# Decays as steps of the written SSD order, transposed tiles scaled on VectorE from PSUM, and layer norm sums between the last group's steps

## The chip, the cores and the metric

The kernel runs on one core of a Trainium2 chip. The core has engines that each work through their own instructions in order and wait for one another by semaphores: TensorE (PE in the profile, with its weight loads shown as PEld), VectorE (DVE), ScalarE (ACT), GpSimd (POOL), and SyncE (SP), which issues most DMA transfers. The metric is the device time of one execution, in microseconds (us), lower being better. Matmuls write to PSUM, a small memory that DVE and ACT read; everything else on the chip lies in SBUF.

## The reference

One step of a decoder layer for 336 tokens of width 1024: a prompt of 272 (16 learned meta tokens and 256 new ones) and 8 running sequences of 8 tokens each (64 sample tokens). Cut to what this case touches:

```
proj = rmsnorm(x) @ w_in + b_in            # glu_in, z, xbc, dt, gates
u    = ga * sigmoid(gb)                     # conformer branch
c    = depthwise31(concat(cache, u))        # 31 taps per channel
y_a  = silu(layernorm(c)) @ w_conf_out + b_conf_out
xbc  = silu(depthwise4(concat(cache, xbc))) # x (32 heads x 64), B, C (8 groups x 128)
# SSD of a chunk, per group of 4 heads
decay  = exp(where(causal, acs[t] - acs[s], -inf))   # acs = cumsum(dt * A)
y_diag = (C @ B^T * decay) @ (dt * x)
y_off  = (C @ h) * exp(acs)
h      = exp(acs[last]) * h + B^T @ (exp(acs[last] - acs) * dt * x)
y   = (y_diag + y_off + D_skip * x) * silu(z)
y_b = group_rmsnorm(y) @ w_m_out
x   = x + (sigmoid(g_a) * y_a + sigmoid(g_b) * y_b) @ w_o
x   = x + peer(rmsnorm(x))                  # 8 heads x 16 of 16384 experts
```

The outputs are the tokens, the last 30 convolution inputs, the last 3 short convolution inputs and the SSD states.

## The kernel before

Activations lie transposed: channels on the 128 partitions, the 336 tokens in the columns (first the 64 sample tokens, then the 272 of the prompt). The prompt's tokens and the sample's are cut into three tiles, `TILES = ((0, 80), (80, 128), (208, 128))`: the first holds the sample and the 16 meta tokens, the others a chunk of 128 each.

**Projections.** One call of `proj` makes 128 output channels. It keeps 32-bit accuracy by splitting activations and weights into a high and a low part: 8 x 2 matmuls with the high weights `wh` on the parts `ah` and `al`, then 8 with the low weights `wl` on `ah`, 24 in all, into a PSUM buffer of tag pj (3 buffers). `weight` loads 512 KB (`wraw`, 4 buffers), casts it to `wh` on ACT (L214) and subtracts to `wl` on POOL (L215; of some weights on DVE), with 2 buffers each.

**Groups.** The SSD has 8 groups of 4 heads. For each group the main loop makes two projections of the Conformer branch (`conf`: value and gated), four of `xbc` (two of x, then B, then C, each followed by the short convolution and Silu) and two of `zproj` (Silu to `sz`). The long convolution of 31 taps (`conv_long`) runs its first tap on ACT (L391) and 30 on DVE (L393), on the prompt's and the sample's columns apart: 60 DVE instructions a group. The short one (`conv_short`) has one tap on ACT (L406) and three on DVE (L408).

**SSD steps.** `ssd(g, ...)` is a generator; the main loop advances it between projections, each `yield` being such a place:
- `turn(i)` transposes x and B of tile i on PE into a PSUM buffer of tag misc (ptr; the tag has 2 buffers, shared with pcb, pst, pq and the pst2 of `update`); ACT copies B out (L530) and scales x by dt in four pieces of 64 columns (L532); POOL makes `wx` of it.
- `inner(i)` makes C B^T (pcb), and DVE multiplies the decays `dec` with it in place (L545).
- `state(i)` makes the new chunk state: pst on PE; DVE copies it (tile 0, L553) or adds to it the old state times its decay, in four pieces (L557).
- `running()` reads the 8 sample states `st` (a DMA of 1 MB a group) into pq, and POOL scales `st` (eight products, L569). `update(q)` adds the new part to them: four matmuls into two PSUM buffers, then two additions on DVE (L599), in two steps, `update(0)` and `update(2)`.
- `out(b)` makes the output of two heads: py and po in PSUM buffers of tag y (2 buffers), then DVE (L585, L587, the latter with the growth factors `e2`) and POOL.
- The last step makes the sum of squares of the group norm: `sq` on ACT, one matmul (pgn), one addition on DVE (L641) to the running sum `pgn`.

**Decays.** `decays(g)` makes `dec` and `e2` of a group: for each of four heads two matmuls into a buffer of tag y (L498, L499), then three Exps on ACT, one a tile; then for each two heads two matmuls (L506) and an Exp (L195) to `e2`. It is called in the main loop between the first and the second xbc projection of the group, and before the loop for group 0. Its matmuls are not pinned.

**What sets the order.** `mm` and `tr` record a matmul or transpose and, inside the main loop, pin it to program order. Matmuls called directly are placed by the scheduler, which orders the rest by a simulated timeline and by priority. All table functions on ACT (Exp, Silu, Sigmoid, Ln; helper `act`, L195) are chained in program order, too, so that table loads are few. Where the next function lies in another table, an ACT_TABLE_LOAD stands between. The rest of DVE's, ACT's and POOL's work is ordered by the scheduler; the long convolution of groups after 0 has low priority.

**After the groups.** In the last group (g = 7) no further xbc projections follow; in their place `gate(0)` to `gate(5)` are projections of the gates, and the layer norm over the Conformer channels begins: `norm_mean` (a sum over the 8 tiles of `cbuf` by a matmul with ones, the eight subtractions on DVE, eight squares on ACT), `norm_var` (eight matmuls with ones) and `norm_scale` (rs on DVE and ACT, then eight products on DVE, L696, and eight Silus on ACT). `gnorm_stats` makes the factors of the group norm from `pgn` (Ln and Exp on ACT, short DVE steps); `gnorm` spreads them by a matmul with `id3` into pgb. Then come the output projections (`conf_out` first) and the expert mixer, which the diff does not touch.

## Time and profile before

| | |
|---|---|
| median of 3 runs | 1510.69 us (1509.24 to 1513.67) |
| profiled execution, its own time | 1508.3 us |
| span of its trace | 1506.5 us |
| mean granted TensorE clock | 0.957 |
| busy: PE | 1356.1 us (90%) |
| busy: PEld | 1272.0 us (84%) |
| busy: DVE | 1008.8 us (67%) |
| busy: ACT | 540.2 us (36%) |
| busy: POOL | 575.2 us (38%) |

Busy times are sums over the span of one profiled execution; the time of an execution is the span and a little around it (1508.3 - 1506.5 = 1.8 us). Rows of a group of instructions read "line engine operation out<-in, shape, count | busy us, mean ns of one | idle us of the engine ahead of them and what ended most of it". Rows of a timeline read "start us, duration us, engine, line, operation, shape, count", and in brackets how long the engine had waited and for whom. A granted clock of 1 is full speed. Tile names are cut to their letters in most rows (`id` is `id3` or `identb`, `acs` both the cumulated sums and their stacked form `acs3`).

### The profile page before, as it was taken

The page shows a single profiled execution, that of the slowest core. Times are in us where ns is not written, and L with a number is a line of the kernel's source. Part 1 is how long each engine was busy: PE and PEld are TensorE (multiplying, and loading weights), DVE is VectorE, ACT ScalarE, POOL GpSimd, SP SyncE. Part 2 cuts the span into 40 slices and gives each one's busy share as a digit, 9 for nine tenths or more (in the row PEclk, how much of TensorE's full clock was granted, in tenths as well). Part 3 has the DMA queues.
Part 4 walks back from the last instruction along what each step waited for, and adds up shares of the span by engine and source line. Part 5 has one row for each costly group of instructions (what it writes and reads, how often), then busy time and mean ns, then how long its engine had stood idle before and what let it go on. Part 6 is the DMA issues. An engine that isn't in the chain of part 4 may idle for free.

```text
span 1506.5 us, 24647 instructions
## 1 busy us (share of the span) xinstructions
PE 1356.1 (90%) x9308; PEld 1272.0 (84%) x9308; DVE 1008.8 (67%) x2350; ACT 540.2 (36%) x1441; POOL 575.2 (38%) x467
## 2 busy tenths in 40 slices
PE   5878877977979799999999988999988999987997
PEld 3767766866867699998989987999988999987997
DVE  6765675675582751256999997677788868776423
ACT  4666566576564744343422222112111101111001
POOL 2236545645656366575322133213223112242100
PEclk9879889989989899999999999999999999999999
DMA  5414234234333234444499989999999999999983
GB/s 192 153 61 158 83 120 165 74 133 144 106 127 113 74 131 148 142 143 158 141 394 414 414 331 416 415 403 364 417 380 417 409 368 375 383 417 416 413 333 104
DMA packets 86807, 382.05 MB, mean 254 GB/s; under 512 B 10112, under 2 KB 15360, under 8 KB 66080
## 3 DMA queue, kind: packets, MB, share of 16 engines
q1 hardware_dynamic: 64144, 226.87, 41.2%
q0 software_dynamic: 20736, 151.00, 24.6%
q10 hardware_dynamic: 1808, 2.60, 0.5%
q8 instruction: 73, 1.20, 0.3%
q14 instruction: 46, 0.38, 0.1%
HBM read 367.41 MB, written 13.03 MB: 253 GB/s over the span
## 4 chain that ended last, share of the span: by engine, by line
PE 49%; DVE 12%; DMA 7%; ACT 1%; issue 1%; POOL 0%; DVEq 0%; POOLq 0%; ACTq 0%
PE va L1277 18%; PE pj L150 14%; PE pj L1186 10%; PE pg L1215 4%; DMA eraw<-in_vE_dram 3%; DMA eraw<-in_uT_dram 3%; DVE ygat L1120 2%; DVE wuv L1112 2%; DMA nd<-x1d 1%; DVE si L922 1%; DVE cand L965 1%; PE psc L1022 1%; DVE si L919 0%; DVE cand L959 0%; DVE cand L962 0%
## 5 line engine op out<-in xcount | busy, mean ns | idle before, releaser
L1000 POOL DMA_INDIRECT wuv<-in_peer_uv_dram,gid x144 | 180.1, 1251 | 513.0 <-DVE ygat L1120 221.8
L215 POOL TENSOR_TENSOR wl<-wraw,wh 128x1024 fp32r<-128x1024 f32 x115 | 275.3, 2394 | 262.4 <-PE pj L150 125.5
L1186 PE MATMUL pj<-nd,eraw 128*128 128x176 f32 x2048 | 321.5, 316 | 12.0 <-DMA eraw<-in_uT_dram 9.1
L1277 PE MATMUL va<-S,eraw 128*128 128x176 f32 x2048 | 315.2, 314 | 12.7 <-DMA eraw<-in_vE_dram 12.7
L1186 PEld LDWEIGHTS pj<-nd,eraw 128*128 128x128 f32 x2048 | 308.0, 191 | 16.2 <-ACT S L1188 7.6
L1277 PEld LDWEIGHTS va<-S,eraw 128*128 128x128 f32 x2048 | 306.1, 190 | 17.6 <-DMA eraw<-in_vE_dram 15.9
L150 PE MATMUL pj<-ah,wh 128*128 128x336 f32 (+1 forms) x768 | 260.0, 346 | 2.1 <-ACT xnf L195 2.1
L150 PE MATMUL pj<-al,wh 128*128 128x336 f32 (+1 forms) x768 | 250.6, 333 | 0.0
L214 ACT CAST wh<-wraw 128x1024 fp32r<-128x1024 f32 x128 | 134.5, 1050 | 200.5 <-PE pj L150 120.9
L1120 DVE SCALAR_TENSOR_TENSOR ygat<-wuv,scg,ygat 128x1024 f32<-128x1024 f32 x128 | 164.0, 1281 | 50.8 <-ACT scg L1115 50.6
L1112 DVE SCALAR_TENSOR_TENSOR wuv<-wuv,x2m 128x1024 f32<-128x1024 f32 x128 | 156.0, 1219 | 40.2 <-DMA wuv<-in_peer_uv_dram,gid 40.2
L1114 ACT ACTIVATE scg<-scg 128x1 f32<-128x1 f32 x144 | 29.1, 202 | 411.5 <-DVE wuv L1112 411.4
L150 PEld LDWEIGHTS pj<-ah,wh 128*128 128x128 f32 x768 | 156.8, 204 | 15.1 <-issue 5.9
L150 PEld LDWEIGHTS pj<-al,wh 128*128 128x128 f32 x768 | 156.6, 204 | 1.0 <-DVE al L215 0.5
L393 DVE SCALAR_TENSOR_TENSOR pcv<-ccat,vec,pcv 128x272 f32<-128x272 f32 x464 | 146.6, 392 | 9.8 <-ACT pcv L391 9.8
L150 PE MATMUL pj<-ah,wl 128*128 128x336 f32 (+1 forms) x768 | 138.4, 319 | 0.0
L150 PEld LDWEIGHTS pj<-ah,wl 128*128 128x128 f32 x768 | 122.7, 189 | 0.8 <-issue 0.7
L1188 ACT ACTIVATE S<-pj 128x176 f32<-128x176 f32 x128 | 37.5, 311 | 148.0 <-PE pj L1186 148.0
L1215 PE MATMUL pg<-oh 128*128 128x64 bf16 x1056 | 75.7, 241 | 0.0
L1215 PEld LDWEIGHTS <-oh 128*128 128x128 bf16 x1056 | 71.2, 117 | 2.3
L1222 DVE TENSOR_TENSOR S<-S,pg 128x192 f32<-128x192 f32 (+1 forms) x66 | 31.6, 507 | 56.7 <-PE pg L1215 56.6
L498 PE MATMUL pdec<-acs,id 96*128 96x336 bf16 x32 | 11.9, 375 | 58.6 <-ACT dec L195 58.5
(345 smaller groups left out, 1750.4 us busy)
## 6 DMA issues: line engine op xcount, KB each, us to landing
eraw<-in_uT_dram SPq DMA_DIRECT2D x128, 512.0 KB, 13.2
eraw<-in_vE_dram SPq DMA_DIRECT2D x128, 512.0 KB, 9.3
wraw<-in_w_in_dram SPq DMA_DIRECT2D x80, 512.0 KB, 3.6
st<-in_state_dram SPq DMA_DIRECT2D x8, 1024.0 KB, 5.2
out_ssm_s_dram<-st SPq DMA_DIRECT2D x8, 1024.0 KB, 6.5
wraw<-in_w_mo_dram SPq DMA_DIRECT2D x16, 512.0 KB, 3.4
wraw<-in_w_q_dram SPq DMA_DIRECT2D x16, 512.0 KB, 3.4
wraw<-in_w_co_dram SPq DMA_DIRECT2D x8, 512.0 KB, 3.5
```

Of the source, the lines that this page charges most:

```text
L150: i_ = nc.tensor.matmul(*a_, **kw)
L214: (nc.vector.tensor_copy if on_dve else nc.scalar.copy)(h, src)
L215: (nc.gpsimd if on_pool else nc.vector).tensor_tensor(l, src, h.bitcast(F32), op=OP.subtract)
L393: t = nc.vector.scalar_tensor_tensor(o, i_, wv, a_, op0=OP.mult, op1=OP.add)
L1000: i_ = nc.gpsimd.indirect_dma_start(out=u, out_offset=None, in_=ia["peer_uv"], in_offset=bass.IndirectOffsetOnAxis(ap=gid[:, c:c + 1], axi ...
L1112: nc.vector.scalar_tensor_tensor(u[:, :D], u[:, :D], 1.0, x2m if c < NPICK else x2e, op0=OP.mult, op1=OP.mult, accum_out=w)
L1120: nc.vector.scalar_tensor_tensor(a_, u[:, D:], scg[:, c:c + 1], a_, op0=OP.mult, op1=OP.add)
L1186: i_ = nc.tensor.matmul(p[:, :ND], raw[:, k, :], nd[:, k, :], start=(k == 0), stop=(k == KD - 1))
L1188: nc.scalar.activation(Sv(b), p[:, :ND], AF.Gelu)
L1215: i_ = nc.tensor.matmul(pg[:, q, :], B[:, q // 4, :, q % 4], A[:, c_, q // 4, :, q % 4], start=(c_ == 0), stop=(c_ == 2))
L1222: nc.vector.tensor_tensor(sv_, sv_, pg.rearrange("p t i -> p i t")[:, i0:i1], op=OP.mult)
L1277: i_ = nc.tensor.matmul(va[k // 2][:, k % 2], raw[:, k, :], Sv(b), start=False, stop=(b == 127), skip_group_check=True)
```

## The change

1. **Decays.** `decays(g)` is gone. Its matmuls and Exps are now steps of `ssd(g)`: `decay(r)` for a head and `growth(b)` for two heads, their matmuls recorded with `mm` and so pinned. Decays 0 and 1 are the first step of a group, decays 2 and 3 come behind `turn(0)`, the growths behind `turn(1)` and `turn(2)`. `dec` and `e2` have one buffer in place of two.
2. **Steps.** The step list of a group is cut anew: decays 0, 1 | turn 0, decays 2, 3 | turn 1, 2, growths | running, inner 0 | inner 1, state 0 | inner 2, state 1, Bm | state 2, out 0 | out 1 | update 0 | update 2 | sum of squares. The main loop advances old and new group alike: the old group's `update(0)` and the new one's first step stand ahead of the value projection, then after each projection one step of each, as far as there are any.
3. **Transposed tiles.** The scaling of x by dt is one product on DVE that reads PSUM, 256 columns, with dt broadcast over 64 columns a head, in place of four ACT instructions. ACT still copies B out.
4. **States.** In `state(i)`, i > 0, POOL multiplies the old state with its decay, and one DVE addition of 256 columns adds PSUM, in place of four DVE instructions.
5. **Last group.** It takes the same steps; `norm_mean` comes before `gate(4)` as it did, `norm_var` is cut into two halves around `gate(5)`, `norm_scale` follows at once, then `gate(6)` and the group's last steps. `gnorm_stats` is called after the loop, and so behind the Silus of the layer norm in ACT's table order; it was called inside `norm_scale`, ahead of them.

```diff
 
-        def decays(g):
-            dec = sp.tile([128, 4, T], F32, name="dec", bufs=2)
-            e2 = sp.tile([128, 2, T], F32, name="e2", bufs=2)
-            for r in range(4):
-                h = 4 * g + r
-                pb = ps.tile([128, T], F32, name="pdec", tag="y", bufs=2)
-                nc.tensor.matmul(pb, id3[:, h:h + 1].to_broadcast([3 * H, 128]), acs3, start=True, stop=False)
-                nc.tensor.matmul(pb, identb, mneg, start=False, stop=True)
-                for i, (t0, L) in enumerate(TILES):
-                    act(dec[:, r, t0:t0 + L], pb[:, t0:t0 + L], AF.Exp, bias=acs[i][:, h:h + 1])
-            for b in range(2):
-                pb = ps.tile([128, T], F32, name="pdec", tag="y", bufs=2)
-                for r in range(2):
-                    h = 4 * g + 2 * b + r
-                    nc.tensor.matmul(pb[r * 64:(r + 1) * 64], id3[:, h:h + 1].to_broadcast([3 * H, 64]), acs3,
-                                     start=True, stop=True)
-                act(e2[:, b], pb, AF.Exp)
-            return dec, e2
-
         def r4(ap):
...
 
-        def ssd(g, xg, bc, sz, dec, e2):
+        def ssd(g, xg, bc, sz):
             BT, CT = bc[:, 0, :], bc[:, 1, :]
...
             xt, wx, hs = [], [], []
+            dec = sp.tile([128, 4, T], F32, name="dec")
+            e2 = sp.tile([128, 2, T], F32, name="e2")
+
+            def decay(r):
+                h = 4 * g + r
+                pb = ps.tile([128, T], F32, name="pdec", tag="y", bufs=2)
+                mm(pb, id3[:, h:h + 1].to_broadcast([3 * H, 128]), acs3, start=True, stop=False)
+                mm(pb, identb, mneg, start=False, stop=True)
+                for i, (t0, L) in enumerate(TILES):
+                    act(dec[:, r, t0:t0 + L], pb[:, t0:t0 + L], AF.Exp, bias=acs[i][:, h:h + 1])
+
+            def growth(b):
+                pb = ps.tile([128, T], F32, name="pdec", tag="y", bufs=2)
+                for r in range(2):
+                    h = 4 * g + 2 * b + r
+                    mm(pb[r * 64:(r + 1) * 64], id3[:, h:h + 1].to_broadcast([3 * H, 64]), acs3,
+                       start=True, stop=True)
+                act(e2[:, b], pb, AF.Exp)
 
...
                 nc.scalar.copy(x_[:L, 256:], p[:L, 256:])
-                for r in range(4):
-                    nc.scalar.activation(x_[:L, r * P:(r + 1) * P], p[:L, r * P:(r + 1) * P], AF.Copy,
-                                         scale=dtok[i][:L, 4 * g + r:4 * g + r + 1])
+                nc.vector.tensor_tensor(r4(x_[:L, :256]), r4(p[:L, :256]),
+                                        dtok[i][:L, 4 * g:4 * g + 4, None].to_broadcast([L, 4, P]), op=OP.mult)
                 w_ = sp.tile([128, 4, P], F32, name=f"wx{i}")
...
                 else:
-                    for r in range(4):
-                        c_ = slice(r * P, (r + 1) * P)
-                        nc.vector.scalar_tensor_tensor(h_[:, c_], hs[-1][:, c_], el[:, 8 + i, 4 * g + r:4 * g + r + 1],
-                                                       p[:, c_], op0=OP.mult, op1=OP.add)
+                    nc.gpsimd.tensor_tensor(r4(h_), r4(hs[-1]), decay_b(8 + i), op=OP.mult)
+                    nc.vector.tensor_tensor(h_, h_, p, op=OP.add)
                 hs.append(h_)
...
 
+            decay(0)
+            decay(1)
+            yield
             turn(0)
+            decay(2)
+            decay(3)
+            yield
             turn(1)
+            turn(2)
+            growth(0)
+            growth(1)
             for s_ in range(2):
...
             yield
-            turn(2)
+            running()
             inner(0)
...
             inner(1)
-            inner(2)
-            yield
             state(0)
-            running()
             yield
+            inner(2)
             state(1)
-            state(2)
-            nc.sync.dma_start(oa["ssm_p"][g], hs[2])
             Bm = sp.tile([S0, 4, N], F32, name="Bm")
...
             yield
+            state(2)
+            nc.sync.dma_start(oa["ssm_p"][g], hs[2])
             out(0)
...
 
-        def norm_var():
-            pv.append(pj())
-            for k in range(KD):
+        def norm_var(ks):
+            if not pv:
+                pv.append(pj())
+            for k in ks:
                 mm(pv[0], ones, squares[k], start=(k == 0), stop=(k == KD - 1))
...
             rstd_of(rs, pv[0], D, tp)
-            r24.append(gnorm_stats())
             for k in range(KD):
...
             f()
-        de = decays(0)
         lm[0] = LM[0]
...
         for g in range(G):
-            new = ssd(g, *tiles, sz, *de)
+            new = ssd(g, *tiles, sz)
             if g + 1 < G:
-                ca, cg = conf(g + 1)
-                ca()
-                run(old, 1)
-                run(new, 1)
-                cg()
-                run(old, 1)
-                run(new, 1)
                 tiles, steps = xbc(g + 1)
-                steps[0]()
-                run(new, 1)
-                de = decays(g + 1)
-                steps[1]()
-                run(new, 1)
-                steps[2]()
-                run(new, 1)
-                steps[3]()
+                tasks = conf(g + 1) + steps
+            else:
+                lm[0] = LM[1]
+                tasks = [lambda: gate(len(gates))] * 4
+            run(old, 1)
+            run(new, 1)
+            for f in tasks:
+                f()
+                run(old, 1)
                 run(new, 1)
+            if g + 1 < G:
                 sz, zsteps = zproj(g + 1)
...
                 zsteps[1]()
-                run(new, 1)
                 old = new
             else:
-                lm[0] = LM[1]
-                gate(0)
-                run(old, 2)
-                run(new, 2)
-                gate(1)
-                run(new, 2)
-                gate(2)
-                run(new, 1)
-                gate(3)
-                run(new, 1)
                 norm_mean()
...
                 run(new, 1)
+                norm_var(range(4))
+                run(new, 1)
                 gate(5)
                 run(new, 1)
-                norm_var()
-                run(new, 2)
+                norm_var(range(4, KD))
+                norm_scale()
+                gate(6)
+                run(new, 3)
         nc.scalar.dma_start(oa["mconv"], mnew)
...
         m2 = mix.enter_context(tc.tile_pool(name="m2", bufs=1))
-        norm_scale()
+        r24.append(gnorm_stats())
         while len(gates) < NB:
```

How this moves instructions shows in the order in which each engine takes them.

On PE the place is the start of a group, between its first Conformer projection (value, the rows ahead) and its second (gated, the rows behind). `pst` with a number is the `update(2)` of the group before, `ptr` the transposes of `turn(0)`, `pdec` the decays with their operands `id` and `mneg`. Before, the decays between them are two of the next group's, where the scheduler put them:

```order
L150 MATMUL pst_1269<-wx_734,Bm 128x256
L150 MATMUL pst_1270<-wx_734,Bm 128x256
L498 LDWEIGHTS id_256
L498 MATMUL pdec<-acs_247,id_256 128x336
L499 LDWEIGHTS identb
L499 MATMUL pdec<-mneg,identb 128x336
L498 LDWEIGHTS id_256
L498 MATMUL pdec<-acs_247,id_256 128x336
L499 LDWEIGHTS identb
L499 MATMUL pdec<-mneg,identb 128x336
L155 MATMUL ptr<-cst,xg 80x128 x2
L155 MATMUL ptr<-cst,bc 80x128
```

And of the change:

```order
L150 MATMUL pst_1239<-wx_712,Bm 128x256
L150 MATMUL pst_1240<-wx_712,Bm 128x256
L155 MATMUL ptr<-cst,xg 80x128 x2
L155 MATMUL ptr<-cst,bc 80x128
L150 LDWEIGHTS id_256
L150 MATMUL pdec<-acs_247,id_256 128x336
L150 LDWEIGHTS identb
L150 MATMUL pdec<-mneg,identb 128x336
L150 LDWEIGHTS id_256
L150 MATMUL pdec<-acs_247,id_256 128x336
L150 LDWEIGHTS identb
L150 MATMUL pdec<-mneg,identb 128x336
```

The transposes stand right behind the update now, where two decays stood between them; decays 2 and 3 stand behind the transposes.

On ACT the place is the decays' Exps. Before, they come behind the Silu of an xbc tile `xg`, whose short convolution begins with the first row:

```order
L406 ACTIVATE pj<-mcat,vec 128x360
L195 ACT_TABLE_LOAD
L195 ACTIVATE xg<-pj 128x272
L195 ACTIVATE xg<-pj 128x64
L195 ACT_TABLE_LOAD
L195 ACTIVATE dec<-pdec,acs_199 128x80
L195 ACTIVATE dec<-pdec,acs_224 128x128
L195 ACTIVATE dec<-pdec,acs_240 128x128
```

Of the change, `sz` being the output of a zproj projection and `xt` the copy of B in `turn(0)`:

```order
L195 ACTIVATE sz<-pj,vec 128x336
L637 ACTIVATE sq<-xg 128x336
L195 ACT_TABLE_LOAD
L195 ACTIVATE dec<-pdec,acs_199 128x80
L195 ACTIVATE dec<-pdec,acs_224 128x128
L195 ACTIVATE dec<-pdec,acs_240 128x128
L195 ACTIVATE dec<-pdec,acs_199 128x80
L195 ACTIVATE dec<-pdec,acs_224 128x128
L195 ACTIVATE dec<-pdec,acs_240 128x128
L214 CAST wh<-wraw 128x1024
L417 COPY ccat<-ccache 128x8x30
L529 COPY xt_1252<-ptr 80x128
```

The first two decays' Exps stand behind the last Silu of zproj and ahead of the copy of the first transposed B; those of decays 2 and 3 come after that copy.

On DVE the place is the end of a long convolution (L393) and the update of the states `st` behind it. Before:

```order
L587 TENSOR_TENSOR yo<-po,e_925 128x336
L599 TENSOR_TENSOR st<-st,pst_1794 128x512
L599 TENSOR_TENSOR st<-st,pst_1795 128x512
L599 TENSOR_TENSOR st<-st,pst_1833 128x512
L599 TENSOR_TENSOR st<-st,pst_1834 128x512
L641 TENSOR_TENSOR pgn<-pgn 8x336
L477 SCALAR_TENSOR_TENSOR ccat<-pj,vec,xnf 128x272
L478 SCALAR_TENSOR_TENSOR ccat<-pj,vec,xnf 128x8x8
L545 TENSOR_TENSOR dec<-dec,pcb 80x4x80
L393 SCALAR_TENSOR_TENSOR pcv<-ccat,vec,pcv 128x272
```

Of the change:

```order
L393 SCALAR_TENSOR_TENSOR cbuf<-ccat,vec,pcv 128x64
L595 TENSOR_TENSOR st<-st,pst_1790 128x512
L595 TENSOR_TENSOR st<-st,pst_1791 128x512
L530 TENSOR_TENSOR xt_1803<-ptr,dtok_193 80x256
L644 TENSOR_TENSOR pgn<-pgn 8x336
L477 SCALAR_TENSOR_TENSOR ccat<-pj,vec,xnf 128x272
L478 SCALAR_TENSOR_TENSOR ccat<-pj,vec,xnf 128x8x8
L530 TENSOR_TENSOR xt_1940<-ptr,dtok_218 128x256
L530 TENSOR_TENSOR xt_1949<-ptr,dtok_234 128x256
L393 SCALAR_TENSOR_TENSOR pcv<-ccat,vec,pcv 128x272
```

The three scaled tiles (L530) stand between the states' additions and the next convolution's first DVE step, and `inner(0)` (L545) has left this place.

More of the change, by code (lines that the diff above doesn't have):

```diff
@@ L610, in ssd @@
             inner(1)
+            state(0)
+            yield
             inner(2)
-            yield
-            state(0)
-            running()
-            yield
             state(1)
-            state(2)
-            nc.sync.dma_start(oa["ssm_p"][g], hs[2])
             Bm = sp.tile([S0, 4, N], F32, name="Bm")
@@ L730, in body @@
         for g in range(G):
-            new = ssd(g, *tiles, sz, *de)
+            new = ssd(g, *tiles, sz)
             if g + 1 < G:
-                ca, cg = conf(g + 1)
-                ca()
+                tiles, steps = xbc(g + 1)
+                tasks = conf(g + 1) + steps
[6 more added lines that the diff above has]
+                f()
                 run(old, 1)
                 run(new, 1)
-                cg()
-                run(old, 1)
-                run(new, 1)
-                tiles, steps = xbc(g + 1)
-                steps[0]()
-                run(new, 1)
-                de = decays(g + 1)
-                steps[1]()
-                run(new, 1)
-                steps[2]()
-                run(new, 1)
-                steps[3]()
-                run(new, 1)
+            if g + 1 < G:
                 sz, zsteps = zproj(g + 1)
```

## Prediction

> **What bounds the kernel now.** I read the busy times by stage first, then the waits of the groups, then the timeline of one group.
>
> ```profile
> span 1506.5 us, 24647 instructions
> 69.40:128.60 59.20, 46.68 (x287) 40.80 (x285) 39.45 (x117) 39.58 (x109) 28.25 (x30) 0.83 0.28 89
> 128.60:456.60 328.00, 276.26 (x1773) 236.42 (x1772) 207.23 (x573) 202.55 (x537) 179.65 (x173) 0.91 0.37 123
> 456.60:517.20 60.60, 47.85 (x298) 39.73 (x298) 30.28 (x58) 31.75 (x64) 31.67 (x25) 0.93 0.32 107
> 534.60:780.00 245.40, 239.97 (x1541) 233.02 (x1541) 139.27 (x466) 99.84 (x189) 134.21 (x75) 0.98 0.49 170
> 780.00:1506.50 726.50, 679.31 (x5076) 666.64 (x5074) 530.44 (x1013) 116.74 (x430) 174.90 (x138) 0.99 0.95 379
> ```
>
> The stage rows come from the view of busy times by stretch: length, then busy us of PE, PEld, DVE, ACT and POOL, the granted clock, the DMA share and GB/s. I cut where the second zproj projection of a group ends on PE. From 534.6 us on PE is busy 94 to 98% at a clock of 0.98 or more, and nothing of the diff runs there. What the diff touches lies before: group 0 (59.2 us), groups 1 to 6 (328.0 us, **54.67 each**) and group 7 with the norms. In groups 1 to 6 PE is busy 84%, at a clock of 0.91; DVE (63%), ACT (62%) and POOL (55%) are far from full. Something waits. The view of waits over the groups names it, the timeline tells why:
>
> ```profile
> PE pdec L498 <- ACT dec L195: 55.3, 7, 8.5
> 154.08 0.44 PE L498 MATMUL pdec<-acs,id 96*128 96x336 bf16 x1 [7.89 <-ACT dec L195]
> ...
> 146.63 0.65 ACT L406 ACTIVATE pj<-mcat,vec 128x360 f32<-128x360 f32 x1
> 151.38 0.51 ACT L195 ACTIVATE xg<-pj 128x272 f32<-128x272 f32 x2 [2.80 <-DVE pj L408]
> 151.89 1.28 ACT L195 ACT_TABLE_LOAD   x1
> 153.19 1.57 ACT L195 ACTIVATE dec<-pdec,acs 128x80 f32<-128x80 f32 x6
> ...
> 150.75 0.59 DVE L408 SCALAR_TENSOR_TENSOR pj<-mcat,vec,pj 128x360 f32<-128x360 f32 x1
> 151.25 8.90 DVE L393 SCALAR_TENSOR_TENSOR pcv<-ccat,vec,pcv 128x272 f32<-128x272 f32 x29
> ```
>
> PE's third decay matmul needs a buffer of tag y, and that comes free when ACT has exponentiated the first decay. ACT's table order puts this Exp behind the Silu of the xbc step just projected; the Silu waits for the short convolution on DVE (its last step at 150.75), and a table load follows. PE stands 7.89 us, seven times in all (55.3 us). It pays again afterwards:
>
> ```profile
> 156.89 0.65 PE L150 MATMUL pj<-ah,wh 128*128 128x336 f32 x1
> 162.65 0.69 PE L150 MATMUL pst<-wx,xt 16*128 16x256 f32 x2
> ...
> 184.46 0.42 PE L150 MATMUL pj<-ah,wh 128*128 128x336 f32 x1
> 188.37 1.13 PE L150 MATMUL pst<-wx,Bm 32*128 32x256 f32 x8
> 190.27 0.41 PE L155 MATMUL ptr<-cst,xg 128*80 128x128 f32 x2
> ```
>
> The projection after the stall takes 162.65 - 156.89 = 5.76 us, a later one 188.37 - 184.46 = 3.91, 0.16 us a matmul: 1.85 us more. The eight decay matmuls between stall and projection (154.08 to 156.89) take 2.81 us; at 0.15 each they would be 1.2: 1.6 more.
>
> **The change, part by part.** *Decays as pinned steps.* Decays 0 and 1 now follow the last zproj projection, and an update, the conf value projection, a second update and the first transposes come before decays 2 and 3 ask for the buffers. ACT reaches the Exps 0.5 (Silu of sz) + 1.28 (table) after that projection and is through both at 1.8 + 2 x 1.57 = 5 us. PE asks after 1.1 + 0.6 + 3.9 + 1.1 + 0.8 + 0.5 = 8 us. The stall is covered by 3 us, and with it goes the low clock: 7.89 + 1.85 + 1.6 = 11.3 per group. PE's own work is then 54.67 - 11.3 = **43.3 us**.
>
> What it adds is a wait: the first transposes follow update(2) at once, and need the buffer that DVE's addition to st frees. Today decays fill that gap; the update starts at 188.37, has 1.13 us, and ptr starts at 190.27: 0.8 us to wait, 44.1. Behind ptr on PE stand decays 2 and 3 and the gated projection.
>
> *What is late next* is a ring off PE: first transposes, ACT up to the start of the long convolution, its 60 steps on DVE, the additions to st behind them in DVE's order, the next transposes.
>
> ```profile
> 190.83 0.26 ACT L530 COPY xt<-ptr 80x128 f32<-80x128 f32 x1 [2.55 <-PE ptr L155]
> 198.62 0.44 ACT L391 ACTIVATE pcv<-ccat,vec 128x64 f32<-128x64 f32 x1
> L532 ACT ACTIVATE xt<-ptr,dtok 128x64 f32<-128x64 f32 x64 | 14.9, 328 | 0.0
> L195 ACT ACTIVATE e<-pdec 128x336 f32<-128x336 f32 x16 | 7.3, 455 | 1.9 <-PE pdec L506 1.9
> L557 DVE SCALAR_TENSOR_TENSOR hs<-hs,el,pst 128x64 f32<-128x64 f32 x64 | 13.3, 277 | 7.7 <-PE pst L150 7.7
> L545 DVE TENSOR_TENSOR dec<-dec,pcb 128x512 f32<-128x512 f32 x16 | 10.8, 681 | 5.0 <-PE pcb L150 5.0
> L553 DVE COPY hs<-pst 128x256 f32<-128x256 f32 x8 | 3.4, 424 | 8.3 <-PE pst L150 8.2
> L569 POOL TENSOR_TENSOR st<-st,el 128x256 f32<-128x256 f32 x64 | 36.9, 615 | 0.0
> ```
>
> From ptr (190.27) to the end of the second pcv start (199.06) pass 8.8 us now. Out go twelve scaled copies (14.9/64 each: 2.8); in come two pairs of Exps (3.1), a table load (1.28) and two e2 Exps (0.9): 11.3. Then DVE: 60 steps at 8.90/29 = 0.307 (18.4), twelve short steps at the 0.5 from 150.75 to 151.25 (6.0), three products with dec (two at 0.68, a smaller one some 0.5: 1.85), a copy and two state additions (3 x 0.42), four output operations on 336 columns (some 0.52 each, between 0.42 and 0.68: 2.1), two additions to st (512 columns, 1.35): 31.0. With 0.8 for the addition that frees the buffer the ring takes 43.1 us, against 44.1 on PE. PE stays the bound, by one microsecond, and DVE's order puts the end of the convolution just ahead of that addition. I add 0.9 us for short waits (an estimate; bounds 0 and 3.9, one projection held back once a group): **45.0 us per group**.
>
> *Transposed tiles on VectorE, states with GpSimd.* ACT loses L532, counted above. DVE loses eight L557 (13.3/64 each: 1.7) and gains three products and two additions on 256 columns. The trace has no product from PSUM with such a broadcast; its bounds are the 0.42 of L553 and the 0.68 of L545, 2.1 to 3.4 for five. I take 0.42, the same number of columns. The three products come before the convolution starts, so 1.3 to 2.0 beside ACT's work there: 0, with +2 a group if that cover is gone. The states' products cost POOL 2 x 0.615, and POOL is idle 24 us in a group. DVE's addition waits for them, with convolution steps queued behind it; by the order they stand behind a weight split on POOL that ends, by my count, 1.5 us before DVE asks. Cost 0, bounds 0 and +1.5.
>
> *Group 0.*
>
> ```profile
> 72.70 0.44 PE L498 MATMUL pdec<-acs,id 96*128 96x336 bf16 x1 [3.12 <-ACT dec L195]
> 75.50 0.65 PE L150 MATMUL pj<-ah,wh 128*128 128x336 f32 x1
> 80.93 0.38 PE L155 MATMUL ptr<-cst,xg 128*80 128x128 f32 x2
> ```
>
> It holds the decays of groups 0 and 1 now. Out: 8.5, 1.85 and 1.6 as above, the second set's own 1.8, the 3.12 shown, 1.6 on its decays and 5.43 - 3.91 = 1.5: 20.0. In: two decays that lie before 69.4 now (0.6) and 1.7 of waits. 59.2 becomes 41.5, a gain of **17.7**.
>
> *Group 7 and the norms.*
>
> ```profile
> 465.91 0.44 PE L155 MATMUL ptr<-cst,xg 128*128 128x128 f32 x2 [0.49 <-ACT xt L532]
> 468.03 0.40 PE L150 MATMUL pcb<-bc 128*80 128x80 f32 x2 [1.57 <-ACT xt L532]
> 468.19 0.60 PE L150 MATMUL pj<-ah,wh 128*128 128x336 f32 x1
> 473.51 0.60 PE L150 MATMUL pcb<-bc 128*128 128x128 f32 x4
> 488.17 6.33 DVE L696 TENSOR_TENSOR cbuf<-cbuf,rs 128x336 f32<-128x336 f32 x8 [1.04 <-ACT rs L694]
> 504.38 0.73 PE L150 MATMUL pgn<-sq,cstm 128*8 128x336 f32 x2 [0.87 <-DVE st L599]
> 517.21 0.72 PE L150 MATMUL pgb<-acs,id 96*128 96x336 bf16 x2 [8.18 <-DVE acs L225]
> ```
>
> In: its own decays (1.8), the ptr wait (0.8). Out: the waits on L532 (0.49 + 1.57) and the slow projection behind them (473.51 - 468.19 - 3.91 = 1.4). The eight subtractions (6.33) now stand on DVE ahead of a dec product that PE needs: +1.3 by my count. The norm's 16 sum matmuls cost what they cost. The stall before pgb stays, and its cover goes: gate(6) ran inside it, now it runs ahead, and ACT has its evacuation (0.5), a table load, eight Silus (some 0.55 each) and two more loads with Ln and Exp (3.5) to do before nine short DVE steps (4.4): 14.1 us from gate(6)'s end to pgb, 2.9 of them PE's work. That is 11.2 idle against 0.87 + 8.18 now: +2.2. Together **+2.6**, bounds -3 and +6.
>
> **Sum.** 17.7 + 6 x (54.67 - 45.0) = 58.0, less 2.6: 73 us. The profiled execution took 1508.3 us (its span and 1.8 around it): 1435. The median of the runs, 1510.69, lies 2.4 above it: **1437**.
>
> [...]
>
> **Rivals.** *(a) New waits in the ring.* ACT and DVE run in a fixed order, one microsecond off the path; one late cast or weight split moves all. At 48 us a group: 14.7 + 6 x 6.67 - 2.6 = 52, **1458**. For it the thin margin, against it that ACT idles 20 us in a group. *(b) Short waits in a cluster lower the clock,* as at 468: 1.4 us in each of seven groups, 10, **1447**. *(c) The stall only moves:* the Silu of C's tile holds the Exps at the new place, too. It would have to be late by 3 us after two further projections to be seen, by 11 to undo the gain: **1510**. *(d) Slower.* DVE's state addition waits for POOL's product, which stands behind weight splits and the eight products with st (8 x 0.615 = 4.9 us); taps, short steps and so Silus and pj buffers stand behind the addition. Each microsecond beyond the 1.5 of cover costs one in each of seven groups. The gain is gone at 10.4; with 13 it is 18 us slower, **1529**. POOL's 24 idle us speak against it.
>
> **Chances.** Forecast 0.64 (own range 1428 to 1447), (a) 0.20, (b) 0.08, (c) 0.04, (d) 0.03, 0.01 for anything else. The range 1424 to 1463 takes in (a) and (b), and at its low end a ring without any wait (44.1, 5 us less) and a group 7 that gains. A measurement of this kernel tells 0.3% (4.5 us) from no change: faster 0.93, same 0.04, slower 0.03.
>
> **What would show it.** Right: no wait of several us at pdec; 45 us from a group's first update to the next group's; 3.9 us for every projection; a granted clock near 1 in groups 1 to 6; 8 to 12 idle us before pgb. Wrong: a period of 48 or more, with PE waiting for a cast, a weight split or a product on DVE; projections of 5 us; or a stretch from the first conf_out to the end that is not 972 us long.

## The result and the profile after

| | before | after |
|---|---|---|
| median | 1510.24 us (4 runs) | 1431.84 us (1431.42 to 1433.83, 4 runs) |
| ratio to before | | 0.948, 95% interval 0.9462 to 0.9497 |
| profiled execution, span | 1506.5 us | 1430.0 us |
| mean granted clock | 0.957 | 0.974 |
| busy PE, DVE, ACT, POOL | 90, 67, 36, 38% | 93, 70, 37, 41% |

The kernel is 78.4 us faster. The view of busy times by stretch, cut at the same events as before (at the end of the second zproj projection that comes ahead of each of groups 0, 1 and 7, at the first pgb and at the first conf_out), shows where. At the first cut the first decay starts in the changed kernel; in the kernel before, two decays (0.6 us) lie ahead of it. The columns are those of the prediction's first fence.

```profile
0.00:72.10 72.10, 51.80 (x259) 42.09 (x260) 49.54 (x104) 36.69 (x87) 16.97 (x21) 0.91 0.49 167
72.10:111.30 39.20, 39.20 (x280) 36.06 (x279) 32.48 (x93) 31.20 (x79) 27.60 (x30) 1.00 0.39 122
111.30:372.40 261.10, 255.29 (x1772) 224.48 (x1772) 204.73 (x562) 190.43 (x467) 188.13 (x188) 1.00 0.47 156
372.40:444.00 71.60, 51.39 (x310) 41.52 (x310) 37.02 (x71) 42.58 (x82) 32.04 (x27) 0.84 0.27 91
444.00:460.80 16.80, 14.75 (x80) 13.87 (x80) 12.93 (x25) 8.94 (x19) 9.66 (x8) 0.86 0.18 53
460.80:1430.00 969.20, 922.18 (x6616) 903.61 (x6614) 670.42 (x1477) 215.99 (x617) 307.91 (x211) 0.98 0.84 327
```

| stretch | before | after | measured | forecast |
|---|---|---|---|---|
| up to group 0 | 69.4 | 72.1 | +2.7 | 0 |
| group 0 | 59.2 | 39.2 | -20.0 | -17.7 |
| groups 1 to 6 | 328.0 | 261.1 | -66.9 | -58.0 |
| group 7, norms, pgb | 78.0 | 88.4 | +10.4 | +2.6 |
| from conf_out on | 971.9 | 969.2 | -2.7 | 0 |

In groups 1 to 6 PE is busy 98% now and its clock is 1.00 throughout. DVE, ACT and POOL are busy there about as long as before (205, 190 and 188 us in place of 207, 203 and 180, the difference being the moved products); what has gone is idle time. The last group got much longer, at a granted clock of 0.84.

The waits of the groups (us in total, times, the longest) hold no row for pdec any more. What PE itself still waits for there are two rows:

```profile
PE ptr L155 <- DVE st L595: 4.6, 6, 0.8
PE ptr L155 <- DVE pgn L644: 0.6, 1, 0.6
```

And this is one group boundary in the timeline, PE first, then ACT, then DVE (start, length, and in brackets the wait and its releaser):

```profile
155.77 0.32 PE L150 MATMUL pdec<-acs,id 96*128 96x336 bf16 x1
...
160.17 1.13 PE L150 MATMUL pst<-wx,Bm 32*128 32x256 f32 x8
162.08 0.42 PE L155 MATMUL ptr<-cst,xg 128*80 128x128 f32 x2 [0.78 <-DVE st L595]
162.44 0.31 PE L150 MATMUL pdec<-acs,id 96*128 96x336 bf16 x1
...
154.91 0.52 ACT L195 ACTIVATE sz<-pj,vec 128x336 f32<-128x336 f32 x1
155.44 1.28 ACT L195 ACT_TABLE_LOAD   x1
156.73 1.58 ACT L195 ACTIVATE dec<-pdec,acs 128x80 f32<-128x80 f32 x6
...
158.87 0.68 DVE L393 SCALAR_TENSOR_TENSOR cbuf<-ccat,vec,pcv 128x272 f32<-128x272 f32 x2
161.33 1.29 DVE L595 TENSOR_TENSOR st<-st,pst 128x512 f32<-128x512 f32 x2 [1.78 <-PE pst L150]
162.93 0.42 DVE L530 TENSOR_TENSOR xt<-ptr,dtok 80x256 f32<-80x256 f32 x1 [0.31 <-ACT xt L529]
```

Three things are to be read here. The Exps of decays 0 and 1 end at 158.31, and PE asks for their buffer at 162.44: the stall is covered by 4.1 us. The only wait left here is the 0.78 us of the first transposes for DVE's addition. And DVE ends the long convolution at 159.55, then itself waits 1.78 us for PE's pst: DVE is that far from being the bound here. It is so at five of the seven boundaries; at the first and the sixth DVE waits only 0.26 and 0.57 us.

The last group's timeline, PE first, then DVE:

```profile
406.65 0.70 PE L150 MATMUL pst<-wx,xt 128*128 128x256 f32 x2 [2.10 <-DVE dec L543]
409.83 0.48 PE L150 MATMUL pj<-al,wh 128*128 128x336 f32 x1
421.69 1.13 PE L150 MATMUL pst<-wx,Bm 32*128 32x256 f32 x8
427.83 2.67 PE L150 MATMUL pst<-wx,Bm 32*128 32x256 f32 x8 [5.00 <-DVE st L595]
444.01 0.72 PE L150 MATMUL pgb<-acs,id 96*128 96x336 bf16 x2 [11.96 <-DVE acs L225]
...
398.44 7.55 DVE L699 TENSOR_TENSOR cbuf<-cbuf,rs 128x336 f32<-128x336 f32 x8 [1.39 <-ACT rs L697]
421.59 5.59 DVE L714 TENSOR_TENSOR cbuf<-cbuf,rs 128x336 f32<-128x336 f32 x8
427.10 1.27 DVE L595 TENSOR_TENSOR st<-st,pst 128x512 f32<-128x512 f32 x2
```

`update(0)` ends on PE at 422.82, but DVE has just begun the norm's eight products (421.59, 5.59 us) and adds to `st` only at 427.10. `update(2)` needs the PSUM buffers that this addition frees: 5.00 us. Ahead of it, the eight subtractions hold a decay product back (2.10 us), and before pgb PE stands 11.96 us.

In the kernel before, DVE took these products (L711 there) behind the additions to `st`:

```profile
504.57 0.68 DVE L599 TENSOR_TENSOR st<-st,pst 128x512 f32<-128x512 f32 x1
...
506.78 3.42 DVE L711 TENSOR_TENSOR cbuf<-cbuf,rs 128x336 f32<-128x336 f32 x8
```

They took 3.42 us there. The view of the tile (ns of one: least, median, most) and GpSimd's timeline show where the other 2.2 us of the 5.59 come from:

```profile
L714 DVE TENSOR_TENSOR cbuf<-cbuf,rs x8: 494/496/2652, 421.6 to 426.7; 128x336 f32<-128x336 f32 x8
421.90 2.40 POOL L215 TENSOR_TENSOR wl<-wraw,wh 128x1024 fp32r<-128x1024 f32 x1 [1.88 <-ACT wh L214]
```

One product, from 422.01 to 424.66, took 2.65 us, the others half a microsecond. It falls together with GpSimd's split of the weight for gate(6), which the change has put ahead of the last steps. The same holds for one of the eight subtractions, 2.65 us beside a split at 403.28, and for one in the kernel before, 2.68 us beside a split at 491.76. That the split causes it was not tried by itself.

### The profile page after: what moved, and what is told of

Its sections match the earlier page's. It is cut to its first block, busy times and chain, and to the rows that moved or that the text cites. A ratio compares the mean times of both kernels' runs of the same rounds, so it can differ in the third digit from the quotient of the medians.

```text
span 1430.0 us, 24506 instructions
## 1 busy us (share of the span) xinstructions
PE 1334.6 (93%) x9308; PEld 1261.6 (88%) x9308; DVE 1007.1 (70%) x2326; ACT 525.8 (37%) x1347; POOL 582.3 (41%) x483
## 4 chain that ended last, share of the span: by engine, by line
PE 51%; DVE 13%; DMA 6%; ACT 1%; POOL 0%; issue 0%; DVEq 0%; ACTq 0%
PE va L1267 19%; PE pj L150 14%; PE pj L1176 12%; PE pg L1205 5%; DMA eraw<-in_vE_dram 3%; DVE ygat L1110 2%; DVE wuv L1102 2%; DMA eraw<-in_uT_dram 2%; DVE si L912 1%; DVE cand L955 1%; DMA nd<-x1d 1%; PE psc L1012 1%; DVE si L909 1%; DVE cand L949 1%; DVE cand L952 1%; DVE ci L909 0%
## 5 line engine op out<-in xcount | busy, mean ns | idle before, releaser
L1176 PEld LDWEIGHTS pj<-nd,eraw 128*128 128x128 f32 x2048 | 311.5, 193 | 13.8 <-ACT S L1178 8.5
L150 PE MATMUL pj<-ah,wh 128*128 128x336 f32 (+1 forms) x768 | 250.0, 334 | 2.4 <-ACT xnf L195 2.1
L150 PE MATMUL pj<-al,wh 128*128 128x336 f32 (+1 forms) x768 | 241.3, 322 | 0.0
L1110 DVE SCALAR_TENSOR_TENSOR ygat<-wuv,scg,ygat 128x1024 f32<-128x1024 f32 x128 | 163.9, 1280 | 53.4 <-ACT scg L1105 53.2
L393 DVE SCALAR_TENSOR_TENSOR pcv<-ccat,vec,pcv 128x272 f32<-128x272 f32 x464 | 151.7, 388 | 17.9 <-ACT pcv L391 17.9
L150 PEld LDWEIGHTS pj<-ah,wh 128*128 128x128 f32 x768 | 148.5, 194 | 12.2 <-issue 4.4
L150 PEld LDWEIGHTS pj<-al,wh 128*128 128x128 f32 x768 | 148.7, 194 | 1.1 <-DVE al L215 0.5
L408 DVE SCALAR_TENSOR_TENSOR pj<-mcat,vec,pj 128x360 f32<-128x360 f32 x96 | 56.4, 587 | 0.5 <-ACT pj L406 0.3
```

What stands on the lines that cost most here:

```text
L150: i_ = nc.tensor.matmul(*a_, **kw)
L393: t = nc.vector.scalar_tensor_tensor(o, i_, wv, a_, op0=OP.mult, op1=OP.add)
L408: nc.vector.scalar_tensor_tensor(o, cat[:, w:w + n], wv, o, op0=OP.mult, op1=OP.add)
L1110: nc.vector.scalar_tensor_tensor(a_, u[:, D:], scg[:, c:c + 1], a_, op0=OP.mult, op1=OP.add)
L1176: i_ = nc.tensor.matmul(p[:, :ND], raw[:, k, :], nd[:, k, :], start=(k == 0), stop=(k == KD - 1))
```

## The experiments

Each kernel was timed against the kernel before on the same chip, so the ratios can be compared. The parts of the span that no kernel here edits vary from kernel to kernel: the first decay starts on PE between 68.8 and 72.1 us, and the stretch from the first expert matmul to the end takes 749.3 to 755.8 us. So beside the times stands, for kernels made from the changed one, the **middle stretch** between these two places, 679.6 - 72.1 = 607.5 us in the changed kernel.

### One call moved in the kernel before

```diff
                 steps[0]()
                 run(new, 1)
-                de = decays(g + 1)
                 steps[1]()
...
                 zsteps[1]()
                 run(new, 1)
+                de = decays(g + 1)
                 old = new
```

> The kernel before with one call moved: the decays of the next group are recorded behind its last zproj projection, not between its first two xbc projections; nothing else of the change. Theory A (the gain comes from the place of the Exps in ACT's table order; the rest of the change adds little): the stall of 7.9 us at the third pdec goes; since all six decay buffers now follow one another on PE, short waits of 0.8 to 1.5 us for each Exp set take its place, some 4 us a group; a period of 47 to 50 us, 1460 to 1480 us. Theory B (the new cut of the steps, VectorE and GpSimd carry a good part): the stall only moves, a period of 52 us or more, over 1490 us.

Measured: 1460.1 us, ratio 0.9662 (0.9646 to 0.9678). The period is 47.9 us (pq of group 1 at 143.82, of group 6 at 383.32, five periods). PE at the decays, then in the projection behind them, and the stretches around them with their clock:

```profile
214.63 0.30 PE L498 MATMUL pdec<-acs,id 96*128 96x336 bf16 x1 [1.10 <-ACT dec L195]
215.36 0.30 PE L498 MATMUL pdec<-acs,id 96*128 96x336 bf16 x1 [0.28 <-ACT dec L195]
216.09 0.33 PE L506 MATMUL pdec<-acs,id 96*64 96x336 bf16 x2 [0.28 <-ACT dec L195]
216.83 0.33 PE L506 MATMUL pdec<-acs,id 96*64 96x336 bf16 x2 [0.40 <-ACT dec L195]
217.60 0.48 PE L150 MATMUL pj<-ah,wh 128*128 128x336 f32 x1
```

```profile
214.00:217.10 3.10, 1.50 (x9) 0.62 (x8) 3.10 (x10) 3.10 (x13) 1.11 (x2) 1.00 0.49 166
217.10:220.60 3.50, 3.50 (x15) 3.50 (x14) 0.06 (x1) 0.75 (x3) 0.96 (x2) 0.54 0.11 37
```

One line of the old kernel, with no other part of the change, brings 51 of the 78 us: theory A. The third pdec waits 1.10 us in place of 7.9. What this kernel lacks against the change is also in the rows: four waits of 2.06 us together, and a projection of 5.51 us in place of 3.99, since the clock falls to 0.54 for 3.5 us. That is 3.6 of the 4.4 us between the two periods. The changed kernel, with the decays spread over three places of the step order, shows neither; the spreading alone was not tried. Fewer table loads are not the cause of the gain: this kernel has 27 ACT_TABLE_LOADs at L195 in place of 34, but the changed kernel has 36 and is faster.

### The decays alone put back

```diff
-            decay(0)
-            decay(1)
             yield
             turn(0)
-            decay(2)
-            decay(3)
...
-            growth(0)
-            growth(1)
...
             for n_, f in enumerate(tasks):
+                if n_ == 3 and g + 1 < G:
+                    de = decays(g + 1)
                 f()
```

with `decays(g)` as it was, two buffers each.

> The changed kernel with the decays alone as they were: one function, unpinned, recorded between the first two xbc projections, two buffers each; steps, VectorE scaling, GpSimd states and the last group as in the change. Theory A: the stall of some 7 us at the third pdec is back in each group, with slower projections behind it; a period of 53 to 55 us, 1495 to 1510 us. Theory B: the other parts hold their share, a period under 50 us, below 1475 us.

Measured: 1507.09 us, ratio 0.997 (0.9955 to 0.9986), a period of 53.2 us (pq at 145.46 and 464.92, six periods). PE's third decay, and ACT around it:

```profile
207.03 0.44 PE L498 MATMUL pdec<-acs,id 96*128 96x336 bf16 x1 [6.58 <-ACT dec L195]
...
204.32 0.51 ACT L195 ACTIVATE xg<-pj 128x272 f32<-128x272 f32 x2 [2.04 <-DVE pj L408]
204.84 1.28 ACT L195 ACT_TABLE_LOAD   x1
206.13 1.58 ACT L195 ACTIVATE dec<-pdec,acs 128x80 f32<-128x80 f32 x6
```

The stall is back, with the same neighbours as before: the Exp stands behind the Silu of an xbc tile, and that behind DVE. Steps, VectorE and GpSimd without the decays' new place leave 4 us of the 78. Together with the first experiment this settles what the gain hangs on: the place alone brings 51 us, the rest alone 4, and the other 23 come only with both.

### The transposed tiles on ACT again

```diff
-                nc.vector.tensor_tensor(r4(x_[:L, :256]), r4(p[:L, :256]),
-                                        dtok[i][:L, 4 * g:4 * g + 4, None].to_broadcast([L, 4, P]), op=OP.mult)
+                for r in range(4):
+                    nc.scalar.activation(x_[:L, r * P:(r + 1) * P], p[:L, r * P:(r + 1) * P], AF.Copy,
+                                         scale=dtok[i][:L, 4 * g + r:4 * g + r + 1])
```

> The changed kernel with the transposed tiles scaled by ACT as before (four instructions a tile), the decays in their new place. ACT gets 2.8 us more a group, of it 1.9 ahead of the long convolution. Theory S (the ring has the 1.8 us of slack that the changed kernel's trace shows ahead of DVE's addition to st): a period within 0.5 us, 1430 to 1437 us. Theory P (the ring of the prediction, 1.0 us of slack): 1 to 2 us a group longer, 1440 to 1446 us.

Measured: 1435.24 us (1433.19 to 1436.18), ratio 0.9493 (0.9477 to 0.9509), an interval that overlaps the change's. The period is 43.57 us (pq at 128.32 and 389.74, six periods) against 43.52, the middle stretch 678.6 - 68.8 = 609.8 us, 2.3 longer. That is theory S. With the decays in their new place the VectorE product is worth some 2 us over all groups; the slack of 1.78 us takes the rest. Nearly all of the 2 us lie at the first boundary, where the slack was 0.26 us (pq at 82.78 and 128.32: 45.54 us, against 43.43 in the changed kernel). The wait for DVE's addition is 0.56 us longer there, and PE then runs at a granted clock of 0.51 for 3.4 us (116.3 to 119.7):

```profile
115.90 0.42 PE L155 MATMUL ptr<-cst,xg 128*80 128x128 f32 x2 [1.34 <-DVE st L596]
```

### The states on DVE again

```diff
-                    nc.gpsimd.tensor_tensor(r4(h_), r4(hs[-1]), decay_b(8 + i), op=OP.mult)
-                    nc.vector.tensor_tensor(h_, h_, p, op=OP.add)
+                    for r in range(4):
+                        c_ = slice(r * P, (r + 1) * P)
+                        nc.vector.scalar_tensor_tensor(h_[:, c_], hs[-1][:, c_], el[:, 8 + i, 4 * g + r:4 * g + r + 1],
+                                                       p[:, c_], op0=OP.mult, op1=OP.add)
```

> The changed kernel with the states' products on DVE as before (eight instructions of 64 columns a group in place of two additions and two GpSimd products). DVE gets 0.9 us more a group. Theory S (slack of 1.8 us): no change, 1428 to 1436 us. Rival: GpSimd's products hold DVE up, and without them the kernel is faster by 1 us a group: 1422 to 1427 us.

Measured: 1432.78 us, ratio 0.9486 (0.947 to 0.9502); period 43.54 us, middle stretch 678.0 - 71.3 = 606.7. No difference: GpSimd neither gains here nor holds DVE up. At the first boundary PE has the same wait of 1.34 us as in the experiment above, but the clock stays at 1.00 behind it and the matmuls at 0.32 us:

```profile
118.44 0.42 PE L155 MATMUL ptr<-cst,xg 128*80 128x128 f32 x2 [1.34 <-DVE st L597]
```

### The norm behind the last group's steps

```diff
                 norm_var(range(4, KD))
-                norm_scale()
-                gate(6)
                 run(new, 3)
...
-        r24.append(gnorm_stats())
+        norm_scale()
```

with `gnorm_stats` called inside `norm_scale` ahead of the products, and `gate(6)` by the loop behind it.

> The changed kernel with the norm's products and Silus behind the last group's steps, the group norm's factors ahead of the Silus in ACT's table order and gate(6) behind the steps, as before; norm_var still in two halves. Theory Q (the last group lost 10.5 us because the eight products stand on DVE ahead of the additions to st, and because the stall before pgb lost gate(6) as its cover): the 5.0 us of PE waiting for st and the slow matmuls behind it (1.5) go, the stall before pgb shrinks from 12.0 to some 8: 10 us less, 1419 to 1424 us. Rival (the loss is what the group's own decays and their waits cost): at most 3 us less, 1428 us or more.

Measured: 1427.16 us (1423.55 to 1428.13), ratio 0.9443 (0.9425 to 0.946): half of what was expected. PE, then DVE:

```profile
416.65 2.17 PE L150 MATMUL pst<-wx,Bm 32*128 32x256 f32 x8 [0.77 <-DVE st L595]
429.22 0.45 PE L150 MATMUL pgb<-acs,id 96*128 96x336 bf16 x2 [2.81 <-DVE acs L225]
429.66 0.32 PE L150 MATMUL pj<-al,wh 128*128 128x336 f32 x1
440.45 0.44 PE L150 MATMUL pgb<-acs,id 96*128 96x336 bf16 x1 [6.77 <-DVE xg L660]
...
435.62 0.51 DVE L215 TENSOR_TENSOR cl<-cbuf,ch 128x336 fp32r<-128x336 f32 x1 [4.07 <-ACT ch L214]
436.42 3.02 DVE L215 TENSOR_TENSOR cl<-cbuf,ch 128x336 fp32r<-128x336 f32 x7 [0.29 <-ACT ch L214]
```

Theory Q is right about both causes: the wait for `st` falls from 5.00 to 0.77 us, that before pgb from 11.96 to 2.81. Together 13.4 us. (The 0.77 stay because the two updates now stand one right behind the other; in the kernel before, the 4.79 us of the norm's sum matmuls stood between them. No weight split falls on the products here, and they take 3.44 us.) But `update(2)` still takes 2.17 us, where `update(0)` of the changed kernel takes 1.13, and 6.77 us come back at the fifth pgb, which needs the buffer that the third group's product on DVE frees. In DVE's order the eight splits to `cl` (3.8 us) stand ahead of that product, and they wait 4.07 us for ACT, which is still at Silus, a weight cast, a table load and Sigmoids. The middle stretch is 601.4 us (670.2 - 68.8), 6.1 less.

### Gates 7 and 8 ahead of pgb, conf_out between the pgb matmuls

```diff
-NB = 7
+NB = 9
...
-            if g % 3 == 1 and len(gates) < NG:
-                gate(len(gates))
+            between.get(g, lambda: None)()
...
-        for j in range(NCO):
-            conf_out(j)
+        between = {1: lambda: gate(len(gates)), 3: lambda: conf_out(0), 5: lambda: conf_out(1), 7: lambda: conf_out(2)}
```

on top of the kernel above, the splits to `ch` and `cl` now recorded ahead of the loop over the groups.

> As e5_norm_late, with gates 7 and 8 ahead of the first pgb, where PE stands, and gate 9 and the three conf_out projections between the pgb matmuls in their place. If PE has nothing else to do in that stall: its 8 us go but for three more waits of 1 us at pgb: 5 us less than e5_norm_late, 1413 to 1419 us. Rival (the projections delay ACT's and DVE's chain to pgb by their evacuations and weight casts, or conf_out waits for its casts): no gain over e5_norm_late, 1420 us or more.

Measured: 1420.53 us (1417.47 to 1427.22), ratio 0.9405 (0.9371 to 0.9439), 6.6 us below the kernel above in the median, but the two intervals overlap, and in the profiled execution (1423.56 us) the middle stretch is only 1.0 shorter (669.6 - 69.2 = 600.4). The profile shows why it is not more:

```profile
433.83 0.42 PE L150 MATMUL pj<-ah,wh 128*128 128x336 f32 x1 [1.38 <-ACT wh L214]
441.89 0.65 PE L150 MATMUL pj<-ah,wh 128*128 128x336 f32 x1 [3.79 <-ACT wh L214]
```

The waits for pgb are gone, and PE waits for weight casts that stand behind ACT's Silus and Sigmoids instead. That is the rival's mechanism, in part: the two theories aren't told apart in the sum.

### The mean behind inner(2)

```diff
-                norm_mean()
                 gate(4)
                 run(new, 1)
-                norm_var(range(4))
-                run(new, 1)
+                norm_mean()
                 gate(5)
                 run(new, 1)
+                gate(6)
+                run(new, 1)
+                norm_var(range(4))
+                run(new, 1)
                 norm_var(range(4, KD))
-                run(new, 3)
+                run(new, 2)
```

on top of the kernel above, with gate 9 ahead of pgb, too (`NB = 10`).

> As e6_gates_early, with the mean and its eight subtractions behind inner(2), gates 5 and 6 in the steps and gates 7, 8 and 9 in the stall. The 2.1 us of PE waiting for a decay product behind the subtractions go, and 1.5 us of slow matmuls behind it: 3 to 4 us less than e6_gates_early, 1409 to 1415 us. Rival: the squares and the sum come late and PE waits for them instead: no gain.

Measured: 1417.66 us (1416.07 to 1419.38), ratio 0.9387 (0.9372 to 0.9403), above the 1409 to 1415 us expected; the interval overlaps that of the kernel above. No wait for a decay product is left in the last group; pgb and the first conf_out still wait a little, an output projection 1.79 us:

```profile
432.49 0.44 PE L150 MATMUL pgb<-acs,id 96*128 96x336 bf16 x2 [0.79 <-DVE acs L225]
435.83 0.42 PE L150 MATMUL pj<-ch,wh 128*128 128x336 f32 x1 [0.66 <-ACT wh L214]
455.97 0.42 PE L150 MATMUL pj<-yl,wh 128*128 128x336 f32 x1 [1.79 <-POOL yl L215]
```

The middle stretch is 665.4 - 70.7 = 594.7 us, 5.7 less than in the kernel above and 12.8 less than in the changed kernel: more than the 10.4 that the last group had lost.

### Decays 2 and 3 ahead of the transposes

```diff
-            turn(0)
             decay(2)
             decay(3)
+            turn(0)
             yield
```

in the changed kernel.

> The changed kernel with decays 2 and 3 ahead of turn(0): on PE they fill the 0.78 us in which the transposes wait for DVE's addition. By the changed kernel's trace ACT is through the first six Exps 3.4 us after the last zproj projection and PE asks for the buffer at 6 us, so there is no wait at pdec: 0.7 us a group less, seven times 5 us, 1425 to 1428 us. By the prediction's count (through at 5 us) the cover is 1 us and the result is the same. Rival: the copy of B and the tile behind it come 1.6 us later on ACT, and the ring, not PE, sets the period: no change or up to 5 us slower.

Measured: 1425.97 us (1425.15 to 1428.32), ratio 0.9442 (0.9426 to 0.9458). PE at the boundary:

```profile
156.50 1.13 PE L150 MATMUL pst<-wx,Bm 32*128 32x256 f32 x8
157.56 0.32 PE L150 MATMUL pdec<-acs,id 96*128 96x336 bf16 x1
158.40 0.42 PE L155 MATMUL ptr<-cst,xg 128*80 128x128 f32 x2
```

Neither pdec nor ptr waits. The period is 42.94 us (pq at 125.83 and 383.49, six periods), 0.58 less, the middle stretch 672.2 - 69.0 = 603.2 us, 4.3 less where 5 were expected, and no sign of the ring.

### Both together

The edits of the last two experiments in one kernel.

> e7_mean_late and e8_decay_fill in one kernel. If the two gains have nothing to do with one another (one lies in seven group boundaries, the other behind them): 5 to 6 us less than e7_mean_late, 1411 to 1413 us. If the decays in front of the transposes make the ring the bound, or the last group's steps wait for it: 1416 us or more.

Measured: 1416.43 us (1415.35 to 1417.13, 5 runs), ratio 0.9378 (0.9361 to 0.9395): the lowest median here, but only 1.2 us below the kernel without the moved decays, and above the 1411 to 1413 us expected: by the time alone it would be the other theory (1416 us or more). First and last expert matmul of the first half, first of the kernel with the mean late, then of both edits, tell where the rest is (ns of one: least, median, most; then first and last start):

```profile
L1176 PE MATMUL pj<-nd,eraw x2048: 310/313/659, 665.4 to 1034.1; 128*128 128x176 f32 x187
```

```profile
L1176 PE MATMUL pj<-nd,eraw x2048: 310/313/661, 660.2 to 1032.1; 128*128 128x176 f32 x187
```

The expert mixer begins 5.2 us sooner, and the middle stretch is 660.2 - 70.2 = 590.0 us: 17.5 below the changed kernel's, about the sum of 12.8 and 4.3. PE does not wait at pdec, and at ptr only once, for 0.64 us. So the two gains do add up where they are made, and the other theory's mechanisms do not show. But the first half of the mixer takes 371.9 us in place of 368.7, and the whole from there 754.5 in place of 749.3. No edit touches it, and other kernels here lie at both values; why it differs from kernel to kernel was not tried.

## Why the prediction was right, and where it was not

**The stall and its release: right.** Forecast was that the Exps, once behind the zproj Silu, are covered by the value projection and the two updates around it, and that the low clock and the slow projections go with the stall. Both happened in each of groups 1 to 6 (clock 1.00, 3.99 us a projection), and moving that one call shows it from one side, putting the decays back from the other. The rival that the stall only moves is out.

**The group period: 45.0 forecast, 43.52 measured** (pq at 129.50 and 390.63, six periods). The wait at ptr was forecast as 0.8 and is 0.78. PE's own work is 43.52 - 0.78 = 42.7 in place of 43.3. Two terms were off. One is the price of the decays behind the stall: the prediction took 1.6 us off for eight of their twelve matmuls, but from the start of the decays to what follows them on PE the twelve took 0.84 + 2.80 = 3.64 us before and take 0.48 + 0.46 + 0.41 = 1.35 now, 2.3 less. The other is the 0.9 us added for short waits; apart from a single 0.64 us at one ptr there are none. It was added because the margin looked thin, and the margin came from a misread row: `dec` 1.57 us x6 is the time of six Exps, so of two decays, where the prediction took it for one. ACT is through both at 3.4 us (154.91 to 158.31 above), not 5, the cover is 4.1 us, not 3, and the ring has 1.6 us less on ACT: 43.1 - 1.6 = 41.5. The trace's 1.78 us of waiting ahead of DVE's addition is this slack (43.52 - 1.78 = 41.7), and it swallowed most of the 2.8 us that scaling on ACT puts back. So rival (a), priced on a margin of one microsecond, was too likely at 0.20.

**VectorE and GpSimd: right.** The product from PSUM takes the 0.42 us that was taken from the nearest row. DVE's state addition never waits long for GpSimd (0.72 us in the last group), so rival (d) had no start.

**Group 0: -20.0 against -17.7;** the 1.7 us of waits that were put there did not come, since its transposes follow no update of an older group.

**Group 7: +10.4 against +2.6, outside the bounds given (-3 to +6).** This is the step that failed. The prediction looked at DVE's queue for the eight subtractions (L696 of the kernel before is these, not the products, which are L711; "ahead of a dec product that PE needs: +1.3"; it is 2.10, and the granted clock of 0.50 that follows, 408.0 to 411.2, makes the next projection 4.78 us in place of 3.96), but not for the eight products of `norm_scale`, which the change moves in front of the last three steps as well. They stand ahead of DVE's additions to `st`, and `update(2)` waits 5.00 us behind them and then runs at a granted clock of 0.50 (427.8 to 430.5; 2.67 us in place of 1.13). Of the 5.00, some 2.2 are the product that fell together with GpSimd's split for gate(6), and 0.77 remain without the products. The stall before pgb was priced well, 11.2 against 11.96. Taking the norm out of there ended most of both, and a wait came up at another pgb: each order of DVE's work tried in this stretch holds something back.

**Ahead of group 0 and behind conf_out** 0 was forecast, +2.7 and -2.7 came. From kernel to kernel the start of the first decay varies by 3.3 us and the stretch from the first expert matmul on by 6.5, so neither is put down to the change. That the total lies only 5 us below the forecast is thus partly luck: -11 in groups 0 to 6, +8 in the last, and the other 2 from the median, which was put 2.4 us above the profiled execution and lies 0.1 above it.

**The clock.** The forecast's sum has no price on the clock for the wait of 0.8 us at ptr, and the prediction shows no row for that. In the changed kernel groups 1 to 6 ran at 1.00, so the waits of 0.78 us cost none there. One of 1.34 us was followed by a clock of 0.51 for 3.4 us in one kernel (the tiles on ACT) and by 1.00 in another (the states on DVE). For a cluster of waits rival (b) has a price, 1.4 us, from the projection at 468.19 in the kernel before (clock 0.68 from 468.19 to 473.51, behind waits of 0.49 and 1.57 us). The cluster exists in the first experiment and costs 1.5 us there.

## What to carry to other kernels

Where an engine's functions are chained in program order, a function's place in that chain, not its cost, decides what it waits for (PE's wait for the Exps at pdec was 7.89 us before and is none in the changed kernel): put it behind the one whose inputs are ready first, and ask which PSUM buffers its delay holds. Spread the requests for few buffers between long work that needs none of them. When a step is moved, list on every in-order engine what now stands ahead of the instruction that frees a buffer, all of the step's instructions and not just the first batch, and what the other engines do beside it; and read a row's count before its duration is used.

## What the runs showed of the hardware

The clock fell here without a long wait, and a longer wait could leave it alone. In the first experiment PE was busy 1.50 of 3.10 us (48%), its longest wait 1.10 us, and then ran at 0.54 for 3.5 us. With the tiles on ACT a single wait of 1.34 us, with PE busy for the other 1.96 of 3.30 us (59%, 113.0 to 116.3), was followed by 3.4 us at 0.51; with the states on DVE the same wait at the same place was followed by a clock of 1.00. In the experiment with the norm late, the matmuls behind a wait of 2.81 us took 0.32 us each, as long as at a clock of 1.00. What decided whether the clock fell, no run here shows.

A DVE instruction with two SBUF operands of 128 x 336 took 2.65 us in place of 0.50 where it fell together with a weight split on GpSimd (422.01 and 421.90 in the changed kernel).
